# Strassen's seven half-size products for the gate and up products of a SwiGLU FFN, on one core

## The chip, the cores and the metric

The kernel runs on one core of one Trainium2 chip. The metric is the device time of one execution in microseconds (us); a time given for a kernel is the median of its runs. The engines are named as in the profile: PE is the matrix engine's matmuls, PEld its weight loads, DVE the vector engine, ACT the scalar engine, POOL the GpSimd engine, SP the engine that issues the DMAs here.

## The reference

The program is a trunk of two pre-norm residual layers over one sequence of 1024 tokens with 1024 channels, all in float32. Layer 0 is a Mamba-2 mixer, layer 1 a causal Conformer convolution module; a dense SwiGLU FFN with 2816 hidden channels follows each, and a norm ends the stack.

```python
def swiglu_ffn(u, w_gate, w_up, w_down):
    return (jax.nn.silu(u @ w_gate) * (u @ w_up)) @ w_down

h = x
h = h + mamba2_mixer(rmsnorm(h, ssm_norm), ...)
h = h + swiglu_ffn(rmsnorm(h, ffn_norm[0]), ffn_w_gate[0], ffn_w_up[0], ffn_w_down[0])
h = h + conformer_conv_module(rmsnorm(h, cv_norm), ...)   # two products around a 31-tap depthwise convolution
h = h + swiglu_ffn(rmsnorm(h, ffn_norm[1]), ffn_w_gate[1], ffn_w_up[1], ffn_w_down[1])
return rmsnorm(h, final_norm)
```

## The kernel before

Activations lie with channels on the 128 partitions and tokens along the free dimension. The sequence is cut into two blocks of T = 512 tokens, block 0 and block 1; the residual `h` of each is eight tiles of [128, 512]. Every large product is taken in three fast passes: `split` (L183 to L186) writes a number as a rounded part `hi` (ACT, L185) and the rest `lo` (a subtraction on DVE, or on POOL where `weng` says so, L186), and `gemm` (L206 to L211) adds lo x hi, hi x lo and hi x hi into one PSUM bank. Both the activations (`norm_u` makes `U[b]`, eight pairs) and the weights are split on the chip; `weight` (L188) fetches a tile into one of two staging buffers `wst` through SP's queue and splits it into `whi` and `wlo`, four buffers each.

The FFN is cut into parts. `ffn(l, f0, nf, blocks)` stands for `nf` hidden tiles of 128 channels from tile `f0` of layer `l`. Its first steps are the gate and up products, a pair of steps for each hidden tile: 24 matmuls of 512 columns for each block, then SiLU, product and a split into `hid`. Its last eight steps are the down products, 3 x nf matmuls for each block and output tile `d`, added into `h` at L682; for a block in `done` the square of `h` is added to a running sum for the next norm. `chain` strings parts together: the down products of a part stand behind the first two steps of the next part. The very last part cuts its down products into two token halves, so its matmuls have 256 columns.

SBUF space is given out by hand: `Slots` holds 15 big buffers [128, 4, 512] (8 KB a partition) and 6 small ones, taken from a list in the order in which they were given back. PSUM has eight banks; `bank` deals them out in turn by use.

The order of the work is a list `q` of steps (`Unit`), written out by hand in `run` with `weave` and `put`: first the mixer's eight stages with the input and output projections of other stages between, then FFN parts, the convolution module of block 0 with FFN parts of block 1 as filler (the convolution itself is DVE's work, 31 taps, `conv31`), the module of block 1 with layer 1's FFN of block 0 as filler, and the rest of the FFN, in which the blocks share the weights of some parts. `emit` walks the list. A step's weights are fetched and split one step ahead (`AHEAD`), at a higher priority (`BOOST`). A list scheduler then sets each engine's instruction order before the program runs, from priorities and its own estimate of times; the engines run their queues in that order, held back by semaphores alone.

```python
        c = self.chain((0, 8, 5, [0]), (0, 13, 5, [0]), (0, 0, 4, [0, 1]), (0, 4, 4, [0, 1], [0]))
        q += put(c, *at(n1, (1, 3, 3, 4, 4)))
        n0 = self.norm_u(0, "cv_norm")
```

A norm (`norm_u`, `rstd_a`, `rstd_b`) sums the running squares over the partitions by matmuls of one column (L245), takes the root and the reciprocal on small tiles, spreads them by a product (L269), and then makes the eight tiles of `U[b]` one after the other on DVE (L298) and ACT.

Of the kernel before, what the change touches and what calls it, by code (L numbers as in the profile page):

```python
# [36 lines left out]
NBIG = 15  # L37
# [3 lines left out]
NR = 2  # L41


class Slots:
# [6 lines left out]
    def new(self, name, dt=F32):  # L51
        i = self.free.popleft()
        self.cnt += 1
        t = self.pool.tile(self.shape, dt, tag=f"{self.prefix}{i}", name=f"{name}_{self.prefix}{self.cnt}")
        self.own[id(t)] = (i, t)
        return t

    def drop(self, *ts):
        for t in ts:
            i, _ = self.own.pop(id(t))  # L60
            self.free.append(i)


class Unit:
    """A step of the program: `load` fetches its weights and may be emitted ahead of `run`."""

    def __init__(self, run, load=None):
        self.run, self.load, self.then = run, load, None


def weave(main, fill):
    """The units of `main` in order, with the units of `fill` spread evenly between them."""
# [9 lines left out]
def put(q, *at):  # L82
    """The units of q, with others put in before the given places."""
# [9 lines left out]
def at(units, places):  # L93
    """Pairs for `put`: each unit with its place; the last place is for all that are left."""
# [3 lines left out]
class Trunk:  # L98
    def __init__(self, ctx, tc, io):
# [5 lines left out]
        self.big = Slots(self.cp, "b", NBIG, [P, 4, T])  # L105
        self.small = Slots(self.cp, "s", NSMALL, [P, T])
# [22 lines left out]
    def consts(self):  # L129
        nc, cp = self.nc, self.cp  # L130
        self.par = cp.tile([P, PAR_N], F32, name="par")
# [9 lines left out]
        # le[k, l] = 1 where k <= l; gtr[k, s] = 1 where k > s  # L141
        self.le = cp.tile([P, P], F32, name="le")
# [4 lines left out]
        self.gtr = cp.tile([P, P], F32R, name="gtr")  # L147
        nc.vector.tensor_copy(self.gtr, gt)
        self.small.drop(tmp)
    def selects(self):  # L150
        nc, cp = self.nc, self.cp
        # sel[32 g + h, (q, p)] = 1 where h == q, for the 8 heads of group g
        self.sel = cp.tile([P, 8, 64], F32R, name="sel")
# [9 lines left out]
    def halves(self):  # L163
        nc, cp = self.nc, self.cp
        # halves of the convolution's weights and of the gate norm: silu is taken through tanh
        self.cw = cp.tile([P, 120], F32, name="cw")
# [3 lines left out]
        self.gh = cp.tile([P, 16], F32, name="gh")  # L170
# [3 lines left out]
    def warm(self, n):  # L174
        """Has TensorE's clock up by the time that the first inputs are there."""
# [12 lines left out]
    def weight(self, src, kk, cols=P, into=None):  # L188
        """Loads a [128, kk, cols] tile of weights and splits it, into a big tile if given; returns per-k (hi, lo)."""
# [75 lines left out]
    def rstd_b(self, dg, tag="ss", nz=NZ):  # L265
        """Those diagonals on all partitions: a PSUM bank."""
# [9 lines left out]
    def norm_u(self, b, gname, g0=0, keep=None, pool=()):  # L276
        """u = rmsnorm(h) * g of block b, split into self.U[b]; the factors also go to `keep`, if given."""
# [27 lines left out]
    def raw_u(self, b, gname):  # L305
        """x * g of block b, split, for the products that run ahead of the norm."""
# [16 lines left out]
    # ---------------------------------------------------------------- mixer  # L323
# [11 lines left out]
    def mixer_setup(self):  # L335
# [8 lines left out]
        self.mix_bigs = [self.c_am, self.c_em, self.c_xd, self.c_H, self.c_bc, self.c_ms]  # L344
# [648 lines left out]
```

## Time and profile before

| | before |
|---|---|
| median of 3 runs | 2612.21 us (2611.63 to 2615.15) |
| profiled execution, its span | 2612.1 us |
| median of the runs less that span | 0.1 us |
| PE busy, mean granted clock | 2585.7 us, 0.997 |
| DVE, ACT, POOL busy | 1683.8, 1034.9, 479.8 us |
| matmuls | 11922 |
| data read and written in HBM | 201.86 and 4.19 MB |

The span runs from the first to the last instruction; of the profiled execution no other time is recorded, and what lies around the span is taken as the difference to the median. A busy share is that of the whole span. In a row of a group stand the line, engine and operation, the tile written and the tiles read, the shape, the count, the busy time with the mean of one in ns, and the idle time of the engine ahead of them with what ended it. In a row of a list in order of time stand the start and the duration in us; matmuls are pipelined, so their pace is read from start to start. In the chain of waits each step leads back from what ended last to what released it.

### The profile page before, as it was taken

To read this page: it belongs to the slowest core of one execution; us is meant where nothing else is said; L and a number is where in the kernel's file an instruction comes from. 1 tells how busy PE (TensorE), PEld (TensorE's weight loads), DVE (VectorE), ACT (ScalarE), POOL (GpSimd) and SP (SyncE) were. 2 spreads that over 40 slices of the span, in tenths; PEclk is the share of its full clock that TensorE was granted. 3 is DMA by queue.
4 is the path that set the end of the run, shared out by engine and by line. 5 is a ranking of instruction groups with operands and counts; after the bars stand their busy time and mean duration, and the time that the engine had idled before them with its cause. 6 is when DMAs were issued, how large, how long until landed. Compare 5 with 4: busy or idle time off the path is not lost.

```text
span 2612.1 us, 31342 instructions
## 1 busy us (share of the span) xinstructions
PE 2585.7 (99%) x11922; PEld 2087.3 (80%) x11922; DVE 1683.8 (64%) x2681; ACT 1034.9 (40%) x1865; POOL 479.8 (18%) x441
## 2 busy tenths in 40 slices
PE   8999999999999999999999999999999999999998
PEld 6777887888887888888888888878888888888887
DVE  7888889888889554323258993679995522235335
ACT  5554565555555343221233333543325322123232
POOL 3214211112111000000004444444444000000000
PEclk9999999999999999999999999999999999999999
DMA  4222222222222323211113232222232311113322
GB/s 143 81 65 73 73 60 81 73 73 73 81 65 69 94 88 100 79 41 56 37 61 99 96 97 93 92 91 95 90 98 91 94 55 39 53 57 105 96 92 87
DMA packets 69702, 208.07 MB, mean 80 GB/s; under 512 B 7728, under 2 KB 10032, under 8 KB 69552
## 3 DMA queue, kind: packets, MB, share of 16 engines
q1 hardware_dynamic: 69552, 206.08, 25.3%
q8 instruction: 93, 1.52, 0.3%
q14 instruction: 57, 0.47, 0.1%
HBM read 201.86 MB, written 4.19 MB: 79 GB/s over the span
## 4 chain that ended last, share of the span: by engine, by line
PE 93%; DVE 5%; issue 1%; ACT 0%; DMA 0%; POOL 0%; SPq 0%; DVEq 0%; ACTq 0%
PE p L210 87%; DVE wlo L186 1%; PE p L573 1%; PE p L577 1%; PE p L565 1%; DVE v_s L450 1%; PE p L245 1%; PE p L529 0%; PE p L538 0%; PE p L539 0%; PE p L269 0%; PE p L555 0%; DVE un_s L298 0%; PE p L509 0%; DVE ulo_b L186 0%
## 5 line engine op out<-in xcount | busy, mean ns | idle before, releaser
L185 ACT ACTIVATE whi<-wst 128x512 fp32r<-128x512 f32 (+1 forms) x764 | 470.9, 617 | 1141.3 <-PE p L210 1016.7
L210 PE MATMUL p<-uhi_b,wlo 128*128 128x512 f32 x2296 | 917.0, 400 | 0.6 <-ACT uhi_b L185 0.6
L210 PE MATMUL p<-ulo_b,whi 128*128 128x512 f32 x2296 | 906.1, 395 | 1.3 <-POOL ulo_b L186 1.2
L210 PE MATMUL p<-uhi_b,whi 128*128 128x512 f32 x2296 | 906.3, 395 | 0.0
L186 DVE TENSOR_TENSOR wlo<-wst,whi 128x512 fp32r<-128x512 f32 (+2 forms) x524 | 368.2, 705 | 405.0 <-ACT whi L185 401.0
L210 PEld LDWEIGHTS p<-ulo_b,whi 128*128 128x128 f32 x2296 | 432.2, 188 | 105.2 <-issue 3.0
L210 PEld LDWEIGHTS p<-uhi_b,wlo 128*128 128x128 f32 x2296 | 431.6, 188 | 105.1 <-issue 4.0
L210 PEld LDWEIGHTS p<-uhi_b,whi 128*128 128x128 f32 x2296 | 432.1, 188 | 101.3 <-issue 0.2
L186 POOL TENSOR_TENSOR wlo<-wst,whi 128x512 fp32r<-128x512 f32 x240 | 309.6, 1290 | 885.6 <-ACT whi L185 884.0
L210 PE MATMUL p<-hid_b,whi 128*128 128x512 f32 x1296 | 405.6, 394 | 0.0
L210 PEld LDWEIGHTS p<-hid_b,whi 128*128 128x128 f32 x1296 | 243.4, 188 | 56.7
L210 PE MATMUL p<-hid_b,wlo 128*128 128x512 f32 x648 | 255.1, 394 | 0.0
L682 DVE TENSOR_TENSOR h<-h,p 128x512 f32<-128x512 f32 (+1 forms) x144 | 94.5, 656 | 129.6 <-PE p L210 129.3
L666 DVE TENSOR_TENSOR sg_s<-sg_s,p 128x512 f32<-128x512 f32 x88 | 60.4, 687 | 182.4 <-PE p L210 182.4
L746 DVE SCALAR_TENSOR_TENSOR p<-ci_b,par,p 128x503 f32<-128x503 f32 (+28 forms) x240 | 160.1, 732 | 0.9
L748 DVE SCALAR_TENSOR_TENSOR p<-ci_b,par,p 128x512 f32<-128x512 f32 x232 | 158.0, 747 | 0.3
L210 PEld LDWEIGHTS p<-hid_b,wlo 128*128 128x128 f32 x648 | 121.8, 188 | 28.1
L450 DVE SCALAR_TENSOR_TENSOR v_s<-raw,cw,v_s 128x512 f32<-128x512 f32 x144 | 110.8, 772 | 3.7 <-ACT v_s L448 2.4
L522 POOL TENSOR_TENSOR am_b<-le,dtr 128x512 fp32r<-128x512 f32 x64 | 80.1, 1270 | 173.6 <-PE p L539 172.3
L210 PE MATMUL p<-yh_b,wlo 128*128 128x512 f32 x256 | 106.7, 417 | 0.0
L210 PE MATMUL p<-yh_b,whi 128*128 128x512 f32 x256 | 101.3, 396 | 0.0
L210 PE MATMUL p<-yl_b,whi 128*128 128x512 f32 x256 | 101.2, 395 | 0.0
(192 smaller groups left out, 2466.7 us busy)
## 6 DMA issues: line engine op xcount, KB each, us to landing
wst<-w_gu SPq DMA_DIRECT2D x144, 512.0 KB, 3.6
wst<-w_in SPq DMA_DIRECT2D x80, 512.0 KB, 3.7
wst<-w_pw SPq DMA_DIRECT2D x48, 512.0 KB, 3.6
wst<-w_dn SPq DMA_DIRECT2D x48, 448.0 KB, 3.3
wst<-w_out SPq DMA_DIRECT2D x64, 256.0 KB, 2.6
wst<-w_dn SPq DMA_DIRECT2D x40, 256.0 KB, 2.6
wst<-w_dn SPq DMA_DIRECT2D x16, 320.0 KB, 2.9
h<-xT SPq DMA_DIRECT2D x16, 256.0 KB, 6.3
```

The lines of the kernel that those rows point to most:

```text
L185: self.nc.scalar.activation(hi, src, AF.Copy)
L186: (eng or self.nc.vector).tensor_tensor(lo, src, hi.bitcast(F32), ALU.subtract)
L210: self.nc.tensor.matmul(acc, a, b, start=n == 0, stop=n == tot - 1)
L245: nc.tensor.matmul(st[:, z:z + 1], s[:, z * P:(z + 1) * P], self.ones[:, :1], start=True, stop=True)
L450: nc.vector.scalar_tensor_tensor(v, raw[:, k:k + T], w(k), v, op0=ALU.mult, op1=ALU.add)
L522: nc.gpsimd.tensor_tensor(r4(amh), lb, self.ah[:, z, h4].unsqueeze(2).to_broadcast([P, 4, P]), ALU.mult)
L565: nc.tensor.matmul(O[:, zs(j)], H[:, zs(j)], CT[:, zs(z)], start=True, stop=True)
L573: nc.tensor.matmul(Y[po:po + 64, zs(hh // 2)], self.XDT[z % 2][:, hh * 64:(hh + 1) * 64], E[:, zs(r)], start=True, stop=True)
L666: nc.vector.tensor_tensor(t, t, W.pop(("acc", b, 1)), ALU.mult)
L682: nc.vector.tensor_tensor(h, h, acc, ALU.add)
L746: nc.vector.scalar_tensor_tensor(acc[:, s:], x[:, :T - s], w(s), acc[:, s:], op0=ALU.mult, op1=ALU.add)
L748: nc.vector.scalar_tensor_tensor(acc if s < 30 else c, x[:, T - s:2 * T - s], w(s), acc, op0=ALU.mult, op1=ALU.add)
```

## The change

For a pair of hidden tiles, one block and one of gate and up, the product is [256 hidden x 1024 channels] by [1024 channels x 512 tokens]. Cut in two along each of the three directions it is a 2 x 2 by 2 x 2 block product. Before, it is taken as eight block products (64 K-steps of 128 and 3 passes: 96 matmuls of 512 columns for gate and up together). `seven` takes it as seven products of 128 hidden channels, 512 channels and 256 tokens: 7 x 12 matmuls of 256 columns. The sums of weight blocks are made on POOL for each such product (`sums`), those of the inputs once for a block and a layer (`sums_u`), and the results are put together on DVE from four PSUM banks. Weights and sums are split after the sums are made. The weights of the seven products come in one fetch of 1 MB to a big buffer (`fetch`), and each of `fetch`, `sums`, `w1` to `w4` is placed a given time ahead of the product that needs it: `Unit` gets an estimate `t` of its PE time, and `emit` sorts these early steps in by it (12 x 0.119 us for a product).

27 pairs of hidden tiles are taken in this way, in parts of four tiles (one part of two): layer 0, tiles 0 to 17 of block 0 and 0 to 7 of block 1; layer 1, tiles 14 to 21 of block 0 and 2 to 21 of block 1. The others stay as they were. Parts no longer serve two blocks at once. The order changes with it: block 0's FFN of layer 0 ends ahead of the convolution module, block 1's last parts of it come after the module of block 0, and layer 1's order for the two blocks follows. The norms of the next step are put between the last 16 down products of a chain.

For space there are 17 big buffers and three of half size [128, 4, 256]; the mixer's constants and small tiles move into two of the big buffers, which are given back after the mixer; the convolution's input is kept for one block with a border of 30 columns (`HALO`) instead of both blocks; and the memory set aside for DMA descriptors is 1024 bytes. The layout of `w_gu` in HBM puts the four blocks of a pair side by side.

The diff, cut to its core:

```diff
-NBIG = 15
+NBIG = 17
+NHALF = 3
...
+    def sums_u(self, b):
...
+        def join():
+            st["R"] = [self.big.new("rs"), self.big.new("rs")]
+            for q, r in enumerate(st["R"]):
+                h, l = self.UB[b][2 * q:2 * q + 2]
+                nc.gpsimd.tensor_tensor(r, h.bitcast(F32), l.bitcast(F32), ALU.add)
+            self.TU[b], self.TB[b] = {}, []
...
+        def first():
+            r0, r1 = st["R"]
+            tt(r0[:, :, lo], r0[:, :, lo], r0[:, :, hi], ALU.subtract)
+            nc.gpsimd.tensor_tensor(r0[:, :, hi], r0[:, :, hi], r1[:, :, hi], ALU.subtract)
+            stt(r1[:, :, hi], r0[:, :, lo], -1.0, r1[:, :, hi], op0=ALU.mult, op1=ALU.subtract)
+            tt(r1[:, :, lo], r1[:, :, lo], r1[:, :, hi], ALU.add)
+            keep("t4", r1[:, :, lo])
...
+    def seven(self, b, src, name, done):
...
+        def fetch():
+            W["q"] = self.big.new("wq")
+            nc.sync.dma_start(W["q"].rearrange("p a t -> p (a t)"), src.rearrange("p a k c -> p (a k c)"))
+
+        def sums():
+            q, s = W["q"], self.big.new("ws")
+            W["s"] = s
+            a21 = q[:, 2:3].to_broadcast([P, 2, T])
+            nc.gpsimd.tensor_tensor(s[:, 0:2], q[:, 0:4:3], a21, add)
+            nc.gpsimd.tensor_tensor(s[:, 2], q[:, 0], s[:, 1], add)
+            nc.gpsimd.tensor_tensor(s[:, 3], q[:, 1], s[:, 2], add)
+
+        def pair(n0, n1, x):
+            w = self.big.new("wh", F32R)
+            self.split(w[:, 0:2], w[:, 2:4], x)
...
+        def w1():
+            pair("a11", "a22", W["q"][:, 0:4:3])
...
+        def w3():
+            pair("s3", "s1", W["s"][:, 0:2])
+
+        def w4():
+            pair("s2", "s4", W["s"][:, 2:4])
...
+        def p1():
+            for n in "abcd":
+                A[n] = self.bank2()
+            product("a11", "b11", A["a"][:, :HT])
...
+            nc.scalar.activation(A["v"], A["a"][:, :HT], AF.Copy)
+
+        def p4():
+            product("a22", "t4", A["b"][:, HT:])
+
+        def p7():
+            product("s3", "n3", A["c"][:, :HT])
+
+        def p6():
+            product("s2", "t2", A["b"][:, :HT])
+            tt(A["v"], A["v"], A["b"][:, :HT], add)
+            tt(A["w"], A["c"][:, :HT], A["v"], sub)
+
+        def p5():
+            product("s1", "t1", A["d"][:, :HT])
+            A["x"] = self.half.new("hx")
+            tt(A["x"][:, 3], A["w"], A["d"][:, :HT], sub)
+
+        def p2():
+            product("a12", "b21", A["a"][:, :HT], True)
+            tt(A["x"][:, 2], A["w"], A["b"][:, HT:], add)
+
+        def p3():
+            product("s4", "b22", A["d"][:, :HT], True)
+            tt(A["x"][:, 1], A["v"], A["d"][:, :HT], add)
+            self.small.drop(A.pop("s"))
+            done(A["a"][:, :HT], A["x"])
+        t = 12 * MH
+        return [Unit(p1, t=t, pre=((14, fetch), (9, sums), (4.5, w1))), Unit(p4, t=t),
+                Unit(p7, t=t, pre=((4.5, w3),)), Unit(p6, t=t, pre=((4.5, w4),)), Unit(p5, t=t),
+                Unit(p2, t=t, pre=((4.5, w2),)), Unit(p3, t=t)]
...
+        def up(f, c11, y):
+            b = blocks[0]
+            x = W.pop(("x", f))
+            nc.vector.tensor_tensor(x[:, 0], x[:, 0], c11, ALU.mult)
+            nc.vector.tensor_tensor(x[:, 1:], x[:, 1:], y[:, 1:], ALU.mult)
...
+            self.split(t[:, 0:2], t[:, 2:4], xv)
...
-        c = self.chain((0, 8, 5, [0]), (0, 13, 5, [0]), (0, 0, 4, [0, 1]), (0, 4, 4, [0, 1], [0]))
-        q += put(c, *at(n1, (1, 3, 3, 4, 4)))
+        c = self.chain(fast(0, 0, 4, [0]), fast(0, 4, 4, [0]), fast(0, 8, 4, [0]), fast(0, 12, 4, [0]),
+                       fast(0, 16, 2, [0], [0]), free=0, hold=8)
+        q += put(c, *at(n1, (-16, -14, -12, -10, -8)))
...
+        q += put(p2, *at(self.sums_u(1), (1, 2, 3)))
+        n0 = self.norm_u(0, "ffn_norm", 8)
+        c = self.chain(fast(0, 0, 4, [1]), fast(0, 4, 4, [1], [1]), free=1, hold=8)
+        q += put(c, *at(n0, (-16, -14, -12, -10, -8)))
...
+        c = self.chain(fast(1, 14, 4, [0]), fast(1, 18, 4, [0], [0]), free=0, hold=8)
+        q += put(c, *at(n1, (-16, -14, -12, -10, -8)))
...
+        c = self.chain(self.ffn(1, 0, 2, [1]), fast(1, 2, 4, [1]), fast(1, 6, 4, [1]), fast(1, 10, 4, [1]),
+                       fast(1, 14, 4, [1]), fast(1, 18, 4, [1], [1], True), free=1, hold=1)
+        su = self.sums_u(1)
+        q += put(c, (0, f0[:1]), (1, f0[1:] + su[:1]), (2, su[1:2]), (3, su[2:]), (-7, f1[:1]), (-5, f1[1:])) + f2
...
-    nc = _bacc.Bacc("TRN2", target_bir_lowering=False, num_devices=1)
+    nc = _bacc.Bacc("TRN2", target_bir_lowering=False, num_devices=1, dynamic_dma_scratch_size=1024)
```

More of the change, by code (lines that the diff above doesn't have):

```diff
@@ L41 @@
 NR = 2
+HALO = 30
+TW = HALO + T
+HT = T // 2
+MM = 0.2315
+MH = 0.119
 class Slots:
@@ L51, in new @@
     def new(self, name, dt=F32):
+        assert self.free, [x[2] for x in self.own.values()]
         i = self.free.popleft()
@@ L105, in __init__ @@
         self.big = Slots(self.cp, "b", NBIG, [P, 4, T])
+        self.half = Slots(self.cp, "x", NHALF, [P, 4, HT])
         self.small = Slots(self.cp, "s", NSMALL, [P, T])
@@ L644, in ffn @@
+    def ffn(self, l, f0, nf, blocks, done=(), halves=False, fast=False):
         nc = self.nc
@@ L668, in gu, with gate @@
                 self.small.drop(t)
+        def gate(f, c11, x):
+            W["x", f] = x
+            nc.scalar.activation(x[:, 0], c11, AF.Silu)
+            nc.scalar.activation(x[:, 1:], x[:, 1:], AF.Silu)
+        def up(f, c11, y):
[3 more added lines that the diff above has]
+            nc.vector.tensor_tensor(x[:, 1:], x[:, 1:], y[:, 1:], ALU.mult)
+            t = self.big.new("hid", F32R)
+            hid[b].append(t)
+            xv = x.rearrange("p (m n) c -> p m (n c)", n=2)
+            self.split(t[:, 0:2], t[:, 2:4], xv)
+            self.half.drop(x, y)
         def load_dn(d):
@@ L814, in run @@
                 self.big.drop(*self.LB[b])
-        return [Unit(lambda d=d: run(d), lambda d=d: load(d)) for d in range(KD)]
+        return [Unit(lambda d=d: run(d), lambda d=d: load(d), 24 * MM) for d in range(KD)]
     def final(self, b, part=()):
```

197 lines of the change are left out of this document (136 added, 61 removed).

## The prediction

> **What bounds the kernel now.** I read the page first: the busy shares and the slices, then the shares of the chain of waits.
>
> ```profile
> PE 2585.7 (99%) x11922; PEld 2087.3 (80%) x11922; DVE 1683.8 (64%) x2681; ACT 1034.9 (40%) x1865; POOL 479.8 (18%) x441
> ...
> PE   8999999999999999999999999999999999999998
> PEclk9999999999999999999999999999999999999999
> ...
> PE 93%; DVE 5%; issue 1%; ACT 0%; DMA 0%; POOL 0%; SPq 0%; DVEq 0%; ACTq 0%
> PE p L210 87%; DVE wlo L186 1%; PE p L573 1%; PE p L577 1%; PE p L565 1%; DVE v_s L450 1%; PE p L245 1%; PE p L529 0%; PE p L538 0%; PE p L539 0%; PE p L269 0%; PE p L555 0%; DVE un_s L298 0%; PE p L509 0%; DVE ulo_b L186 0%
> ...
> L210 PEld LDWEIGHTS p<-ulo_b,whi 128*128 128x128 f32 x2296 | 432.2, 188 | 105.2 <-issue 3.0
> ```
>
> TensorE is busy from end to end at the full granted clock, and 87% of the chain is one helper, `gemm` at L210. A busy PE need not be PE at its peak, so next come the longest pieces of the chain in order of time (start, us, what), then one stretch of PE's own list whose matmuls are half as wide, with what follows it, then two stretches of the busy times by window.
>
> ```profile
> 930.77 417.42 PE p L210 x1800
> ...
> 1355.15 273.14 PE p L210 x1176
> ```
>
> ```profile
> 2559.37 22.61 PE L210 MATMUL p<-hid_b,wdn_b 128*128 128x256 f32 x189
> 2581.82 0.50 PE L245 MATMUL p<-onesr,ssum_s 128*128 128x1 f32 x4
> ```
>
> ```profile
> 840.00:1355.00 515.00, 515.00 (x2232) 417.79 (x2231) 208.03 (x336) 145.31 (x244) 0.00 (x0) 1.00 0.23 70
> ...
> 1735.00:1970.00 235.00, 235.00 (x1011) 189.46 (x1010) 207.64 (x307) 76.69 (x126) 110.62 (x86) 1.00 0.30 94
> ```
>
> 1800 matmuls of 512 columns in 417.42 us and 1176 in 273.14 are 0.232 us each. The 189 of 256 columns fill the time to the next instruction, (2581.82 - 2559.37) / 189 = 0.1188 us each. These runs have no hole, so in the FFN a matmul's price is its pace. The windows show the cover: DVE busy 208 of 515 us in the first FFN stretch, and 208 of 235 us under the block-1 convolution, both without PE idling. So nothing but PE is saved or lost here, unless another engine comes late.
>
> **The change, part by part.**
>
> Matmuls. A plain pair of hidden tiles for one block takes 2 tiles x 2 (gate, up) x 24 matmuls = 96 of 512 columns: 96 x 0.232 = 22.27 us. By the seven products it takes 2 x 7 x 12 = 168 of 256 columns: 168 x 0.1188 = 19.96 us. The new order has 27 such pairs: 9 of layer 0 on block 0, 4 on block 1, then 4 and 10 of layer 1. Removed are 2592 wide matmuls (601.3 us), added 4536 narrow ones (538.9 us): -62.4 us. The last part, which is cut in token halves, shrinks from seven hidden tiles to four: 144 narrow matmuls become 72 wide ones, 17.1 against 16.7 us, -0.4 us.
>
> What feeds a seven. One `seven` is 7 x 12 x 0.1188 = 9.98 us of PE. Its other work is priced from these groups (last columns: busy, mean ns) and rows in order of time (start, duration).
>
> ```profile
> L682 DVE TENSOR_TENSOR h<-h,p 128x512 f32<-128x512 f32 x128 | 87.8, 686 | 119.7 <-PE p L210 119.6
> ...
> L682 DVE TENSOR_TENSOR h<-h,p 128x256 f32<-128x256 f32 x16 | 6.7, 419 | 9.9 <-PE p L210 9.8
> ```
>
> ```profile
> 1360.52 2.72 DVE L298 SCALAR_TENSOR_TENSOR un_s<-h,par,p 128x512 f32<-128x512 f32 x4
> ...
> 1363.75 2.49 DVE L186 TENSOR_TENSOR ulo_b<-un_s,uhi_b 128x512 fp32r<-128x512 f32 x4
> ```
>
> ```profile
> L185 ACT ACTIVATE whi<-wst 128x512 fp32r<-128x512 f32 x704 | 443.8, 631 | 1078.2 <-PE p L210 960.3 <-POOL wlo L186 56.0 <-issue 53.4
> ...
> L185 ACT ACTIVATE whi<-wst 128x128 fp32r<-128x128 f32 x20 | 6.1, 310 | 11.1 <-PE p L210 10.2 <-DMA wst<-w_dt 0.2
> ```
>
> ```profile
> 1653.78 1.28 POOL L186 TENSOR_TENSOR wlo<-wst,whi 128x512 fp32r<-128x512 f32 x1 [1.85 <-ACT whi L185]
> 1655.76 1.02 POOL L186 TENSOR_TENSOR wlo<-wst,whi 128x384 fp32r<-128x384 f32 x1 [0.70 <-ACT whi L185]
> ```
>
> A DVE op of 512 columns follows the last after (2.49 - 0.69) / 3 = 0.60 us (0.66 for the scaled form at 1360.52), and a column costs (686 - 419) / 256 = 1.04 ns: 0.33 us for 256 columns, 0.87 for 768, 1.13 for 1024. POOL's column costs (1.28 - 1.02) / 128 = 2.03 ns, so 2.32 us for 1024. ACT's is (631 - 310) / 384 = 0.84 ns, 1.06 us for 1024. Per seven: DVE splits weights (3 of 1024, one of 512: 3.99 us), makes five sums that read PSUM (1.65), and every second seven multiplies 256 and 768 columns and splits 1024 of `hid` (2.33, half is 1.17): 6.8 us. POOL makes the weight sums, 2.32 + 2 x 1.28 = 4.9 us. ACT: 3 x 1.06 + 0.63 for weights, 0.42 for the copy, half of 0.42 + 0.85 + 1.06: 5.4 us. Each is below 9.98, so at full overlap the sevens cost nothing more. But the two SBUF users meet:
>
> ```profile
> 1659.24 1.30 POOL L186 TENSOR_TENSOR wlo<-wst,whi 128x512 fp32r<-128x512 f32 x1 [2.46 <-ACT whi L185]
> ...
> 1669.27 1.30 POOL L186 TENSOR_TENSOR wlo<-wst,whi 128x512 fp32r<-128x512 f32 x1 [1.84 <-ACT whi L185]
> ```
>
> ```profile
> 1655.70 1.28 DVE L790 TENSOR_TENSOR co_b<-co_b,p 128x512 f32<-128x512 f32 x2
> ...
> 1659.89 1.20 DVE L186 TENSOR_TENSOR ll_b<-co_b,lh_b 128x512 fp32r<-128x512 f32 x1
> ...
> 1669.74 1.37 DVE L186 TENSOR_TENSOR ll_b<-co_b,lh_b 128x512 fp32r<-128x512 f32 x1 [1.17 <-ACT lh_b L185]
> 1671.04 0.67 DVE L682 TENSOR_TENSOR h<-h,p 128x512 f32<-128x512 f32 x1
> ```
>
> At 1659.24 and 1669.27 POOL subtracts. DVE's subtraction of two SBUF tiles that begins meanwhile takes 1.20 and 1.37 us instead of 0.69 and ends 0.55 us behind POOL, while the one that reads PSUM (1655.70, two in 1.28 us) overlaps POOL's 1655.76 unharmed. So DVE's two-SBUF-input work, 3.99 + half of 0.87 + 1.13 = 5.0 us a seven, and POOL's 4.9 us take turns: 9.9 of 9.98 us. The Trainium skill ("SBUF — State Buffer", Who interferes with whom) says that the later of two such instructions is blocked until the first is through; the trace agrees, with the 1.37 us. Without that rule DVE would have 3.2 us spare in each seven, the stall below would be near nothing and the sum 2556; with it as the rows show, the sum is the 2575 below.
>
> What is queued behind such a wait: DVE takes its queue in order, and `p3` (bank `d`) may not add to its bank before DVE has read `p5`'s result from it (`x[:, 3]`). Only `p2`, 1.43 us, lies between. DVE is in a two-input op for 5.0 of 9.98 us, and about half of these meet POOL; then the read waits on average half of POOL's 2.32 us, half of DVE's 1.13, and its own 0.33, some 2.0 us, 0.6 past the cover: 0.25 x 0.6 = 0.15 us. I add 0.2 us for weights that reach `p1`, `p7` or `p6` late in the same way (they are called 4.5 us ahead and need 1.06 + 1.13 plus one block): 0.35 us a seven. Bounds: 0, as in the window where DVE is 88% busy and PE never idles; and DVE and POOL strictly in turn, 6.8 + 4.9 = 11.7, 1.7 us a seven. I stay near the lower, dense row. 54 sevens x 0.35 = +19 us (0 to 92).
>
> Loads. Each seven fetches one 1 MB block where 512 KB tiles came before.
>
> ```profile
> wst<-w_gu SPq DMA_DIRECT2D x144, 512.0 KB, 3.6
> ...
> wst<-w_dn SPq DMA_DIRECT2D x40, 256.0 KB, 2.6
> ```
>
> From 2.6 us at 256 KB and 3.6 at 512, 1 MB is some 5.6 us by estimate, and it is issued 14 us ahead, 5 ahead of POOL's sums. Gate/up traffic goes from 144 x 512 KB to 54 x 1 MB and 68 x 512 KB, since block 0 and 1 no longer share splits: 16 MB more; w_dn goes from 104 to 160 issues, 8 MB more. All go through SP's queue, where a fetch waits for a big buffer and the w_dn loads behind it: of 17, inputs and their sums hold 8, `hid` 2, weights up to 6, so one or two are free. At 4.5 to 14 us of lead I put this at 0; if a buffer comes 5 us late the sums do too, which is part of the 1.7 us bound.
>
> Norms. Two waits of the old order go. In its chain between 1655 and 1725:
>
> ```profile
> 1655.53 19.42 PE p L210 x84
> ...
> 1674.97 0.70 DVE h L682
> ...
> 1675.69 0.64 ACT sq_s L223
> ...
> 1676.35 1.23 DVE ssum_s L231
> ...
> 1677.63 1.05 PE p L245 x8
> ...
> 1721.77 0.76 DVE h L811
> ...
> 1724.43 1.05 PE p L245 x8
> ```
>
> PE's products end at 1655.53 + 19.42 = 1674.95, and PE stands until 1677.63 behind the last sum of squares; it stands again from about 1721.75 to 1724.43. Each is 2.7 us, so -5.4 us: the new order has other work between. It has three like places: after the last w_dn product of block 0 and 1 in layer 0 and of block 0 in layer 1, a norm comes at once. A wait there is 0.60 + 0.64 + 0.60 plus hand-overs, 2.1 us. Two I take at that, +4.2 (0 if the matmuls of the next unit are put ahead). The first is worse, because the part ahead of it has two hidden tiles only: 8 w_dn units of 6 matmuls, 11.1 us of PE, against 8 x (0.33 + 0.60 + 0.60) = 12.2 us of DVE. Before these lie 8 units of 12 (22.3 us), with DVE at 2.33 + 8 x 1.20 and the block-1 norm, about 2.6 + 8 x 1.26: 24.6 us. Then come two plain units (11.1 us; DVE 2.4). DVE reaches 39.2 us where PE stands at 44.5, and now the cv norm: 2 us for the sum, the steps that the end of the kernel shows as
>
> ```profile
> 2601.49 0.61 PE L245 MATMUL p<-onesr,ssum_s 128*128 128x1 f32 x4 [1.42 <-DVE ssum_s L231]
> ...
> 2605.07 3.22 DVE L831 SCALAR_TENSOR_TENSOR h<-h,par,p 128x256 f32<-128x256 f32 x8 [0.68 <-PE p L269]
> ```
>
> 3.6 us, then 8 x 1.26: 54.9. The first pw1 product wants its last input at 44.5 + 4.9 (seven eighths of 24 x 0.232) = 49.4, so it is 5.5 us late: +6 (0 to 12).
>
> `sums_u`: POOL joins 2 x 2048 columns (some 9 us), DVE and POOL some 15 more, three times. Twice it lies under 45 us of w_out or pw2; in the last chain under 22 us of plain units with block 0's final norm: +2 (0 to 8). Cover gone, each would cost its 24 us. Constants in two big tiles, the 30-column halo copies (16 on POOL), the convolution moved with its FFN filler: no more work on PE, hidden as the convolution is now; 0, and its cover is the 88%-busy window.
>
> Sum, on the profiled span (2612.1 us, which the median of the runs exceeds by 0.1, so nothing is added around it): -62.4 - 0.4 - 5.4 + 19 + 4.2 + 6 + 2 = -37.0, so **2575 us**.
>
> **The rivals.**
> Slower: DVE and POOL in turn on the shared port. For it: 9.9 of 9.98 us are claimed, and both queues are in order. Against: PSUM readers escape, and the 22 us of w_dn between four sevens let DVE catch up. 54 x 1.7 = 92 in place of 19: 2648. It decides from (37 + 19) / 54 = 1.04 us a seven on. The Trainium skill's page named above speaks for this one. Chance 0.15.
> Halfway: 0.7 to 1.13 us a seven, 2594 to 2617. Chance 0.15, about half of it above 2607.
> All hidden: no new wait; -62.4 - 0.4 - 5.4: 2544, up to 2556 with a few. For it: the 88% window. Chance 0.15.
> The narrow matmuls don't hold 0.1188 us: if every 188 ns weight load showed, 4536 x 0.188 - 601.3 = +251.5 and 2870 us. Against it: the 189 had loads of 188 ns too. Chance 0.03.
> My forecast, 0.1 to 0.7 us a seven: 2556 to 2594. Chance 0.52.
>
> **How the numbers follow.** 0.2% (5 us) is what a measurement can tell. Faster: 0.52 + 0.15 + 0.08; same: 0.07; slower: 0.15 + 0.03. The range 2546 to 2617 drops the two slow cases and a little of the fast one, 0.2 in all; the likeliest's own is 2556 to 2594.
>
> **What the profile would show.** PE's instructions up by 1872, 4536 + 192 matmuls of 128x256 at 0.119 us from start to start. Right: no piece of the FFN chain longer than 0.5 us that isn't PE. Wrong: DVE or POOL in the chain at `seven`'s sums and splits, PE waiting for DVE ahead of `p3`, POOL's adds well over 2.3 us; a hole over 10 us at the first pw1; whi/wh waiting for a DMA.

## The result, and the profile after

| | before, run beside it | after |
|---|---|---|
| median | 2612.03 us (2611.63 to 2615.15) | 2752.73 us (2751.0 to 2754.5) |
| ratio to before | | 1.0533 [1.0519, 1.0548] |
| span of the profiled execution | 2612.1 us | 2752.0 us |
| mean granted clock | 0.997 | 0.966 |

The changed kernel is 141 us slower; 2575 was forecast, faster, with 2617 as the upper end. The page of the changed kernel, the lines that answer to those of before (busy shares, the slices of PE and its clock, the chain by engine and by line, then one issue group):

```profile
PE 2586.6 (94%) x13794; PEld 2191.6 (80%) x13794; DVE 2123.9 (77%) x3072; ACT 1175.8 (43%) x1993; POOL 863.7 (31%) x623
...
PE   8999999999998898889999998999999988998887
PEclk9999999999999999999999998999999999999999
...
PE 71%; DVE 18%; issue 4%; POOL 3%; ACT 3%; DMA 1%; SPq 0%; DVEq 0%; POOLq 0%; ACTq 0%
PE p L226 54%; PE p L749 11%; DVE wh_b L202 5%; DVE wlo L202 2%; POOL ws_b L717 1%; ACT wh_b L201 1%; DVE hid_b L202 1%; DVE v_s L465 1%; DMA wq_b<-w_gu 1%; PE p L588 1%; POOL ws_b L718 1%; PE p L592 1%; PE p L580 1%; DVE em_b L603 1%; DVE un_s L314 1%
...
wq_b<-w_gu SPq DMA_DIRECT2D x54, 1024.0 KB, 4.8
```

PE executes the 1872 instructions more that were foretold, and its share falls from 99% to 94%. DVE rises from 5% of the chain to 18%. `gemm` is now L226, the sevens' product L749. PE is idle for 2752.0 - 2586.6 = 165.4 us, against 26.4 before. Who ends that idle time, from the table of waits of PE (total us, times, longest):

```profile
PE p L749 <- DVE hx_x L776: 104.3, 27, 6.1
PE p L285 <- DVE dgh_s L277: 7.1, 5, 3.0
```

L776 is DVE's read of `p5`'s result (`x[:, 3]`), which `p3` needs before it may use bank `d` again. In 26 of the 27 pairs PE waits for it once, each time at `p3` of the first of the pair's two sevens, for 2.0 to 6.1 us; the 27th wait that is counted, at the `p3` of a second seven, is 0.2 us long. No other wait comes near. One such wait, in order of time (start, duration, idle before and who ended it); first PE, whose `p2` began at 1059.90 and should be followed at once by `p3`:

```profile
1059.90 0.28 PE L749 MATMUL p<-uhi_b,wlo 128*128 128x256 f32 x1
...
1061.21 0.28 PE L749 MATMUL p<-uhi_b,whi 128*128 128x256 f32 x1
1064.64 0.58 PE L749 MATMUL p<-uhi_b,wh_b 128*128 128x256 f32 x1 [3.15 <-DVE hx_x L776]
1065.02 0.41 PE L749 MATMUL p<-ulo_b,wh_b 128*128 128x256 f32 x1
1065.23 0.63 PE L749 MATMUL p<-uhi_b,wh_b 128*128 128x256 f32 x2
...
1067.36 0.47 PE L226 MATMUL p<-hid_b,wlo 128*128 128x512 f32 x1
...
1089.73 0.28 PE L749 MATMUL p<-uhi_b,wh_b 128*128 128x256 f32 x1
```

DVE and POOL in the same stretch:

```profile
1055.73 2.82 DVE L202 TENSOR_TENSOR hid_b<-hx_x,hid_b 128x1024 fp32r<-128x1024 f32 x1 [1.39 <-ACT hid_b L201]
1058.47 2.32 DVE L202 TENSOR_TENSOR wh_b<-wq_b,wh_b 128x1024 fp32r<-128x1024 f32 x1
1060.71 2.30 DVE L202 TENSOR_TENSOR wh_b<-ws_b,wh_b 128x1024 fp32r<-128x1024 f32 x1
1062.93 0.41 DVE L770 TENSOR_TENSOR vw_s<-vw_s,p 128x256 f32<-128x256 f32 x1
...
1064.17 0.41 DVE L776 TENSOR_TENSOR hx_x<-vw_s,p 128x256 f32<-128x256 f32 x1
```

```profile
1055.05 2.41 POOL L717 TENSOR_TENSOR ws_b<-wq_b 128x1024 f32<-128x1024 f32 x1 [14.47 <-DMA wq_b<-w_gu]
1057.54 2.16 POOL L718 TENSOR_TENSOR ws_b<-wq_b,ws_b 128x512 f32<-128x512 f32 x1
1059.78 2.14 POOL L719 TENSOR_TENSOR ws_b<-wq_b,ws_b 128x512 f32<-128x512 f32 x1
```

The two engines alternate to the end of the chain of adds: POOL until 1057.46, DVE's first split until 1058.55, POOL until 1059.70, DVE until 1060.79, POOL until 1061.92, DVE until 1063.01. Each split takes 2.3 to 2.8 us in place of 1.2 (e2 below), and behind the third stand the four small operations that end with L776. `p6` had ended at about 1058.45 (36 matmuls of 0.119 us from 1054.17), so L770, which adds its result, is 4.5 us late. Of what stands ahead of it, two operations are not urgent: the weight splits (`wh_b`) are for the seven that begins at 1089.73, as the current one, which ends at 1067.36, had the last of its weights split by 1046.0. The static order has put them there, 30 us early.

After the pause the matmuls stand 0.21 us apart instead of 0.12 (1065.02 to 1065.23). The windows show the clock (us, PE busy, ..., PEclk, DMA share, GB/s):

```profile
1044.20:1061.30 17.10, 17.10 (x146) 17.08 (x144) 11.25 (x13) 4.87 (x7) 6.09 (x3) 1.00 0.38 139
1061.30:1064.60 3.30, 0.19 (x2) 0.00 (x0) 3.23 (x6) 1.85 (x3) 0.62 (x1) 0.93 0.00 0
1064.60:1069.00 4.40, 4.36 (x19) 4.12 (x20) 2.14 (x3) 0.85 (x1) 1.35 (x1) 0.67 0.21 60
1069.00:1085.00 16.00, 16.00 (x70) 12.93 (x70) 9.81 (x12) 5.81 (x8) 4.51 (x3) 1.00 0.23 66
```

After 3.3 us without a matmul the granted clock is 0.67 on average over the next 4.4 us: 0.50 from 1064.6 to 1067.3, and 1.00 again from 1067.8 on. So a wait costs more than its own length. The Trainium skill ("TensorE: Matmul & The Clock Gate", Part 1) says that an idle window of about 3.4 us brings the clock down to half, and that a matmul then takes its columns over 1.2 GHz, which for 256 is 0.213 us; the trace agrees, with 0.21 us, after a pause a little shorter. The length of the pause alone does not decide it here. In the changed kernel a pause from 2234.8 to 2236.7, which is 2.0 us, was followed first by 1.5 us at the full clock and then by 3.2 us at 0.50; in f3 below, one of 2.7 us that ended at 1719.9 was followed by none (1.00 from 1717 to 1725).

### The profile page after: what moved, and what is told of

It is laid out like the page before. It is cut to its first block, busy times and chain, and to the rows that moved or that the text cites. A ratio compares the mean times of both kernels' runs of the same rounds, so it can differ in the third digit from the quotient of the medians.

```text
span 2752.0 us, 35952 instructions
## 1 busy us (share of the span) xinstructions
PE 2586.6 (94%) x13794; PEld 2191.6 (80%) x13794; DVE 2123.9 (77%) x3072; ACT 1175.8 (43%) x1993; POOL 863.7 (31%) x623
## 3 DMA queue, kind: packets, MB, share of 16 engines
q8 instruction: 108, 1.77, 0.3%
## 4 chain that ended last, share of the span: by engine, by line
PE 71%; DVE 18%; issue 4%; POOL 3%; ACT 3%; DMA 1%; SPq 0%; DVEq 0%; POOLq 0%; ACTq 0%
PE p L226 54%; PE p L749 11%; DVE wh_b L202 5%; DVE wlo L202 2%; POOL ws_b L717 1%; ACT wh_b L201 1%; DVE hid_b L202 1%; DVE v_s L465 1%; DMA wq_b<-w_gu 1%; PE p L588 1%; POOL ws_b L718 1%; PE p L592 1%; PE p L580 1%; DVE em_b L603 1%; DVE un_s L314 1%
## 5 line engine op out<-in xcount | busy, mean ns | idle before, releaser
L201 ACT ACTIVATE whi<-wst 128x512 fp32r<-128x512 f32 (+3 forms) x644 | 395.9, 616 | 834.7 <-PE p L226 631.1
L226 PE MATMUL p<-uhi_b,wlo 128*128 128x512 f32 x1432 | 576.1, 403 | 9.8 <-POOL wlo L202 5.3
L226 PE MATMUL p<-ulo_b,whi 128*128 128x512 f32 x1432 | 566.4, 396 | 2.4 <-POOL ulo_b L202 1.2
L226 PE MATMUL p<-uhi_b,whi 128*128 128x512 f32 x1432 | 565.6, 395 | 0.0
L226 PE MATMUL p<-hid_b,whi 128*128 128x512 f32 x1344 | 423.9, 397 | 0.8 <-DVE hid_b L202 0.8
L226 PEld LDWEIGHTS p<-uhi_b,wlo 128*128 128x128 f32 x1432 | 271.4, 190 | 76.9 <-POOL wlo L202 7.0
L226 PEld LDWEIGHTS p<-ulo_b,whi 128*128 128x128 f32 x1432 | 271.2, 189 | 67.4 <-DVE ulo_b L202 3.2
L226 PEld LDWEIGHTS p<-uhi_b,whi 128*128 128x128 f32 x1432 | 271.0, 189 | 61.4 <-issue 0.2
L749 PE MATMUL p<-tu_b,wh_b 128*128 128x256 f32 x2592 | 317.3, 282 | 0.0
L749 PEld LDWEIGHTS p<-tu_b,wh_b 128*128 128x128 f32 x2592 | 313.3, 191 | 0.0
L749 PE MATMUL p<-uhi_b,wh_b 128*128 128x256 f32 x864 | 209.2, 331 | 104.3 <-DVE hx_x L776 104.3
L226 PEld LDWEIGHTS p<-hid_b,whi 128*128 128x128 f32 x1344 | 256.6, 191 | 58.2 <-DVE hid_b L202 1.1
L226 PE MATMUL p<-hid_b,wlo 128*128 128x512 f32 x672 | 268.4, 399 | 6.0 <-DVE un_s L314 3.2
L749 PEld LDWEIGHTS p<-uhi_b,wh_b 128*128 128x128 f32 x864 | 172.6, 237 | 110.3 <-DVE hx_x L776 109.8
L202 DVE TENSOR_TENSOR wh_b<-ws_b,wh_b 128x1024 fp32r<-128x1024 f32 x108 | 181.7, 1683 | 81.3 <-ACT wh_b L201 81.2
```

The lines of the kernel that those rows point to most:

```text
L201: self.nc.scalar.activation(hi, src, AF.Copy)
L202: (eng or self.nc.vector).tensor_tensor(lo, src, hi.bitcast(F32), ALU.subtract)
L226: self.nc.tensor.matmul(acc, a, b, start=n == 0, stop=n == tot - 1)
L749: nc.tensor.matmul(to, x, y, start=n == 0 and not more, stop=n == 11, skip_group_check=True)
```

## The experiments

All times are medians of the kernel's runs; ratios are to the kernel before, on the same chip. Beside the four groups of runs (the change, e, f with g1, h) the kernel before took 2612.0, 2613.5, 2611.8 and 2612.3 us, so a difference of 2 us between runs of different groups means nothing.

**e1: the new order and space, with plain products**

```diff
-        fast = lambda *a, **k: self.ffn(*a, fast=True, **k)
+        fast = lambda *a, **k: self.ffn(*a, fast=False, **k)
         # and the units of sums_u are left out
```

> The changed kernel with its new order, SBUF plan and weight layout, but with plain products (eight half blocks as 24 matmuls of 512 columns) in place of every seven, and without the sums of inputs. Theory (the loss sits in the sevens alone): the new order costs only its norms, so 2612 plus or minus 15 us, clock 0.99, no PE wait of more than 3 us in the FFN. Rival (the new order, the unshared weights and the tighter SBUF lose it): 2680 us or more.

2599.79 us, ratio 0.9949 [0.9934, 0.9964]. As expected, the order, the halo and the space are not the loss; they gain some 14 us. No wait went for it: PE's idle time is 27.4 us (2598.8 - 2571.4), against 26.4 before, and its busy time fell from 2585.7 to 2571.4. What made these matmuls shorter is open.

**e2: POOL reads no weights.** The sums of weight blocks are left out; POOL writes a constant in their place.

```diff
-            nc.gpsimd.tensor_tensor(s[:, 0:2], q[:, 0:4:3], a21, add)
+            nc.gpsimd.memset(s[:, 0:2], 0.01)
             # the two sums of 512 columns likewise
```

> The sums of weight blocks are left out: POOL fills the same buffers with a constant, so it reads no SBUF in a seven, and the DVE queue keeps its order nearly everywhere. All else is as in the changed kernel. Theory (POOL's adds and DVE's two-input splits block each other on the shared port, DVE comes 3 to 5 us late to the read that p3 waits for, and the pause drops the clock): the 1024-column splits fall from 1.68 us mean to about 1.23, the wait of PE for L776 from 104 us to under 25, the clock rises to 0.99, time 2555 to 2600 us. Rival (DVE is late because splits for later sevens stand ahead in its queue, and wait there for fetches that come late; the port adds little): the wait stays over 70 us and the time over 2690 us.

2575.37 us, ratio 0.9853 [0.9838, 0.9867]: as expected, and 177 us less than the change. The matmuls are the same, and DVE's 3072 instructions, read in order of time, have the same line, tiles and shape at all but 83 places. The groups of 1024-column splits in the changed kernel (last columns: busy, mean ns of one, idle before) and in this one:

```profile
L202 DVE TENSOR_TENSOR wh_b<-ws_b,wh_b 128x1024 fp32r<-128x1024 f32 x108 | 181.7, 1683 | 81.3 <-ACT wh_b L201 81.2
L202 DVE TENSOR_TENSOR wh_b<-wq_b,wh_b 128x1024 fp32r<-128x1024 f32 x54 | 95.5, 1768 | 16.8 <-ACT wh_b L201 16.8
```

```profile
L202 DVE TENSOR_TENSOR wh_b<-ws_b,wh_b 128x1024 fp32r<-128x1024 f32 x108 | 131.7, 1222 | 60.1 <-ACT wh_b L201 59.9
L202 DVE TENSOR_TENSOR wh_b<-wq_b,wh_b 128x1024 fp32r<-128x1024 f32 x54 | 68.1, 1261 | 15.4 <-ACT wh_b L201 15.4
```

A split falls from 1.68 and 1.77 us to 1.22 and 1.26, and the wait at L776 is gone. PE's idle time falls from 165.4 to 51.5 us and its busy time, for equal matmuls, from 2586.6 to 2524.2:

```profile
PE 2524.2 (98%) x13794; PEld 2137.6 (83%) x13794; DVE 1990.3 (77%) x3072; ACT 1173.5 (46%) x1993; POOL 624.9 (24%) x623
```

So the 176.3 us between the two spans are 113.9 of standing still (104.3 of them the wait at L776) and 62.4 of slower matmuls.

**e3 and e4: `p3` in a bank of its own**, in e4 together with e2's edit (the weight sums left out). It costs one more DVE sum and one more bank a seven.

```diff
-            for n in "abcd":
+            for n in "abcde":
...
             tt(A["x"][:, 3], A["w"], A["d"][:, :HT], sub)
+            tt(A["x"][:, 1], A["v"], A["d"][:, :HT], add)
...
-            product("s4", "b22", A["d"][:, :HT], True)
-            tt(A["x"][:, 1], A["v"], A["d"][:, :HT], add)
+            product("s4", "b22", A["e"][:, :HT])
+            tt(A["x"][:, 1], A["x"][:, 1], A["e"][:, :HT], add)
```

> p3 gets a PSUM bank of its own (five banks a seven instead of four) and one more 256-column DVE sum adds p5's result, so p3 no longer waits for DVE to read bank d. Nothing else is taken away; port and queue are as they were. Theory (this one wait, with the half clock behind it, is the whole loss): about 104 us of waits and 80 us of lost clock come back, 2560 to 2610 us. Rival (DVE and POOL are too slow for the sevens, so the wait moves to the next place, weights for p1 and p7 or banks not read yet): 2660 us or more, with as much PE idle time under other names.

> Both edits: p3 in its own bank and POOL writing constants instead of making the weight sums (these are left out). Theory: nothing is left to wait for in the sevens, so the arithmetic gain shows: 2545 to 2575 us, clock 0.99. Rival (late fetches and the norms hold it): 2600 us or more.

e3: 2625.47 us, ratio 1.0048 [1.0033, 1.0063]; e4: 2582.19, 0.9880 [0.9864, 0.9897]. Both expectations were missed: e3 lies between its theory and its rival, and e4 is 7 us above its range. In e3 POOL still holds DVE up as long as before, but PE no longer hangs on it so closely. Its split group and its largest waits:

```profile
L202 DVE TENSOR_TENSOR wh_b<-ws_b,wh_b 128x1024 fp32r<-128x1024 f32 x108 | 180.7, 1674 | 50.9 <-ACT wh_b L201 50.9
```

```profile
PE p L226 <- DVE un_s L314: 11.6, 2, 8.5
...
PE p L749 <- DVE wh_b L202: 7.1, 5, 2.8
```

The same 1.67 us splits then cost 2625.47 - 2582.19 = 43 us rather than 177. The slow splits alone are not the loss; slow splits ahead of the hand-over of one bank are. The edit itself costs 6.8 us (e4 against e2), and the traces show where: the wait of 8.5 us at `un_s` above is the norm behind block 0's FFN, it stands in e4 too (at 1221.3) and in f2, and in e2 PE waits there for less than 2 us. Why the new plan leaves that hole was not traced.

**f1 and f2: the weight sums on DVE**, in f2 with e3's bank.

```diff
-            nc.gpsimd.tensor_tensor(s[:, 0:2], q[:, 0:4:3], a21, add)
-            nc.gpsimd.tensor_tensor(s[:, 2], q[:, 0], s[:, 1], add)
-            nc.gpsimd.tensor_tensor(s[:, 3], q[:, 1], s[:, 2], add)
+            tt(s[:, 0:2], q[:, 0:4:3], a21, add)
+            tt(s[:, 2], q[:, 0], s[:, 1], add)
+            tt(s[:, 3], q[:, 1], s[:, 2], add)
```

> The three sums of weight blocks of each seven move from POOL to DVE; nothing is left out. DVE's own work in a seven rises by 2.3 us to about 9.1 of 9.98. Theory (the shared port, not DVE's amount of work, makes p3 wait): splits of 1024 columns near 1.25 us, PE's wait for L776 under 40 us, clock 0.985 or more, time 2585 to 2635 us. Rival (DVE is simply too full in the sevens): waits of 80 us or more, time over 2670 us.

> The sums on DVE, and p3 in a bank of its own, so that PE no longer waits for the read behind p5 (one more 256-column DVE sum, 9.5 of 9.98 us). Theory: with the port free and the tight wait gone, only input sums and norms are left, 2580 to 2610 us, which beats the kernel before (2612) and perhaps the new order with plain products (2600). Rival (DVE's amount of work binds now): 2630 us or more, PE waiting for weight splits.

f1: 2575.65 us, ratio 0.9863 [0.9848, 0.9878]; f2: 2582.31, 0.9885 [0.9871, 0.9900]. f1 is 9 us below its expected range, f2 within it. Nothing is left out here, and the loss is gone. DVE now carries 6.8 + 1.13 + 2 x 0.60 = 9.1 of 9.98 us a seven by the prediction's prices, and PE does not wait: first block 0's sevens of layer 0 in f1, from the first to the last, then the same stage in the changed kernel (window and us, then PE, PEld, DVE, ACT, POOL busy, PEclk; 1804 of PE's instructions in each):

```profile
914.50:1161.70 247.20, 247.20 (x1804) 233.66 (x1802) 195.07 (x286) 102.37 (x140) 0.00 (x0) 1.00 0.30 98
```

```profile
923.00:1229.50 306.50, 267.39 (x1804) 252.12 (x1803) 197.27 (x236) 102.45 (x140) 104.17 (x50) 0.92 0.24 79
```

So the amount of DVE's work was never the bound. (The scheduler plans anew for f1 and mixes the sums between the reads; in e2, whose order is nearly that of the changed kernel, the loss is gone too.) A run that moves only the read at L776 ahead of the two weight splits, with POOL's sums as they are, was not made; the part that the order plays is read from the rows above and from e3.

**f3: POOL's sums in eight pieces of 256 columns**

```diff
-            nc.gpsimd.tensor_tensor(s[:, 0:2], q[:, 0:4:3], a21, add)
+            for i in range(2):
+                for c in (slice(0, HT), slice(HT, T)):
+                    nc.gpsimd.tensor_tensor(s[:, i, c], q[:, 3 * i, c], q[:, 2, c], add)
             # the other two in halves too
```

> POOL's weight sums in eight pieces of 256 columns instead of one of 1024 and two of 512, with the same columns in all. Theory (each two-input DVE split waits for the POOL instruction that holds the port): a wait ends after some 0.8 us instead of up to 2.4 us, so the splits' mean falls from 1.68 to about 1.45 us and half of the loss against the kernel before comes back: 2660 to 2710 us. Rival (the total time that POOL holds the port decides, and eight pieces hold it longer): no change or slower, 2745 us or more.

2727.45 us, ratio 1.0446 [1.0428, 1.0463], between what the theory and the rival said. A split is held up for less, 1.34 us on average, but it still meets a piece, the pieces take longer in all than the whole sums, and the wait at the read (here L779) stays. The split's group, POOL's groups in the changed kernel and in f3, and f3's largest wait of PE:

```profile
L202 DVE TENSOR_TENSOR wh_b<-ws_b,wh_b 128x1024 fp32r<-128x1024 f32 x108 | 144.3, 1336 | 154.6 <-ACT wh_b L201 154.4
```

```profile
L717 POOL TENSOR_TENSOR ws_b<-wq_b 128x1024 f32<-128x1024 f32 x54 | 145.1, 2686 | 675.6 <-PE p L749 295.3 <-DMA wq_b<-w_gu 141.8 <-PE p L226 118.0
L718 POOL TENSOR_TENSOR ws_b<-wq_b,ws_b 128x512 f32<-128x512 f32 x54 | 100.5, 1861 | 4.2
L719 POOL TENSOR_TENSOR ws_b<-wq_b,ws_b 128x512 f32<-128x512 f32 x54 | 95.5, 1768 | 4.2
```

```profile
L718 POOL TENSOR_TENSOR ws_b<-wq_b 128x256 f32<-128x256 f32 x216 | 227.7, 1086 | 586.6 <-PE p L752 238.4 <-DMA wq_b<-w_gu 120.2 <-PE p L226 113.1
L722 POOL TENSOR_TENSOR ws_b<-wq_b,ws_b 128x256 f32<-128x256 f32 x108 | 120.1, 1133 | 0.0
L720 POOL TENSOR_TENSOR ws_b<-wq_b,ws_b 128x256 f32<-128x256 f32 x108 | 82.1, 781 | 0.0
```

```profile
PE p L752 <- DVE hx_x L779: 92.4, 29, 5.1
```

POOL needs 227.7 + 120.1 + 82.1 = 430 us for the pieces, 341 for the undivided sums. Smaller pieces do not free DVE: 25 us of 177 come back.

**g1, h1, h2: the sums of the inputs.** g1 is e2 without any work in `sums_u`, so it leaves out both kinds of sums; h1 is f1 with what POOL does in `sums_u` on DVE; h2 is the changed kernel with those two alone.

```diff
-                nc.gpsimd.tensor_tensor(r, h.bitcast(F32), l.bitcast(F32), ALU.add)
+                tt(r, h.bitcast(F32), l.bitcast(F32), ALU.add)
...
-            nc.gpsimd.tensor_tensor(r0[:, :, hi], r0[:, :, hi], r1[:, :, hi], ALU.subtract)
+            tt(r0[:, :, hi], r0[:, :, hi], r1[:, :, hi], ALU.subtract)
```

> As the run without POOL reads (weight sums replaced by constants), and the sums of inputs (sums_u) are left out as well: the products read parts of the inputs in their place. The run without POOL reads was 2575 us, 24 us below the plain products in the new order, where the matmuls alone should give 62. Theory (the missing 38 us are sums_u: its POOL adds stand ahead of POOL's weight splits, and its DVE work is in the way of norms): 2540 to 2550 us. Rival (the norms after the short parts and the clock keep it): 2565 us or more.

> The weight sums on DVE as in the run of 2575.7 us, and the three POOL adds of each sums_u moved to DVE too; nothing is left out. In that run POOL's join of 2 x 2048 columns (4.6 and 5.6 us) stands between its weight splits, and PE's chain goes through it at 1441 to 1464 and twice more. Theory (it is the POOL queue that makes sums_u dear, 29 us of which 0 to 8 was foreseen): 2550 to 2562 us, no POOL wlo ahead of PE there. Rival (sums_u costs by its amount of work on DVE and ACT, wherever it stands): 2568 us or more.

> The changed kernel with sums_u on DVE, while the weight sums stay on POOL. Theory (two separate losses: the port in the sevens, some 175 us, and the POOL queue in sums_u, some 20): 2725 to 2740 us. Rival (one loss, and with the port in the way sums_u matters nothing): 2748 us or more.

g1: 2546.07 us, 0.9746 [0.9732, 0.9761]. h1: 2552.35, 0.9766 [0.9752, 0.9779]. h2: 2729.27, 1.0441 [1.0427, 1.0455]. All three came as expected. The two edits give 23.3 us in h1 (against f1) and 23.5 in h2 (against the change): the same, so they are apart from the weight sums. Left out altogether (g1 against e2) the sums give 29.3. What POOL did there is seen in f1 at the first `sums_u`, DVE's rows and POOL's in order of time, and at the second in POOL's alone:

```profile
848.94 4.94 DVE L202 TENSOR_TENSOR wlo<-wst,whi 128x512 fp32r<-128x512 f32 x1 [0.30 <-ACT whi L201]
...
855.00 4.69 DVE L202 TENSOR_TENSOR wlo<-wst,whi 128x512 fp32r<-128x512 f32 x1
```

```profile
848.80 4.53 POOL L670 TENSOR_TENSOR rs_b<-uhi_b,ulo_b 128x2048 f32<-128x2048 f32 x1 [28.18 <-DVE sz_b L623]
854.56 4.58 POOL L670 TENSOR_TENSOR rs_b<-uhi_b,ulo_b 128x2048 f32<-128x2048 f32 x1 [1.23 <-DVE yl_b L202]
```

```profile
1440.75 4.62 POOL L670 TENSOR_TENSOR rs_b<-uhi_b,ulo_b 128x2048 f32<-128x2048 f32 x1 [0.72 <-PE p L226]
1445.33 1.30 POOL L202 TENSOR_TENSOR wlo<-wst,whi 128x512 fp32r<-128x512 f32 x1
1446.58 5.58 POOL L670 TENSOR_TENSOR rs_b<-uhi_b,ulo_b 128x2048 f32<-128x2048 f32 x1
1452.13 1.25 POOL L202 TENSOR_TENSOR wlo<-wst,whi 128x512 fp32r<-128x512 f32 x1
```

A weight split on DVE of 512 columns, 0.69 us elsewhere, meets an add of 2048 columns and takes 4.94 and 4.69 us: it ends 0.55 and 0.55 us behind POOL, as in the window of before. And at 1440 two such adds stand in POOL's queue ahead of weight splits of 1.30 us, so the weights of the product that should hide the adds come late. In f1 PE waits 7.3 us for such splits (0.8 in h1). It waits for DVE as well: behind DVE's meetings with the adds of the last `sums_u` come waits of 3.4 us at `un_s` (2189.1) and 3.4 at `ssum_s` (2217.6), and h1 has neither.

**h3 and h4: the two-tile part first**, in h3 on f1, in h4 on h1.

```diff
-        c = self.chain(fast(0, 0, 4, [0]), fast(0, 4, 4, [0]), fast(0, 8, 4, [0]), fast(0, 12, 4, [0]),
-                       fast(0, 16, 2, [0], [0]), free=0, hold=8)
+        c = self.chain(fast(0, 0, 2, [0]), fast(0, 2, 4, [0]), fast(0, 6, 4, [0]), fast(0, 10, 4, [0]),
+                       fast(0, 14, 4, [0], [0]), free=0, hold=8)
```

> The run of 2575.7 us (weight sums on DVE) with the part of two hidden tiles put first instead of last in block 0's FFN of layer 0, so that the last eight down products are 12 matmuls long and not 6. Theory (the short part leaves DVE behind ahead of the norm of the convolution module, +6 us in the prediction): 2562 to 2571 us. Rival (the wait there has another cause, the first fetches of the next plain part or the norm's own chain): 2573 us or more.

> All three edits together: weight sums and input sums on DVE and the short part first. If the gains add up: 2540 to 2556 us. If they are one and the same slack: as the better one of the two alone.

h3: 2573.85 us (2571.21 to 2574.99) against f1's 2575.65 (2573.76 to 2580.94): no difference that can be told, as the rival said. h4: 2545.71 (2544.75 to 2546.68) against h1's 2552.35 (2550.25 to 2553.37), 6.6 us less; ratio to before 0.9741 [0.9728, 0.9755]. h4 computes everything and is faster than both kernels, 67 us below the one before. The first norm behind block 0's FFN is not what it gains by. In h1's chain this norm is a stretch of short steps of many engines, from 1197.61 (1192.27 + 5.34) to 1211.57:

```profile
1192.27 5.34 PE p L226 x22
...
1211.57 18.63 PE p L226 x80
```

But PE works on other products meanwhile. Its largest wait in h1 between 1140 and 1290:

```profile
PE p L226 <- DVE ulo_b L202: 1.0, 2, 0.8
```

All its waits in that stretch are 1.2 us, the same in f1, and none in h4. From h1 to h4 PE's idle time falls by 5.1 us (37.2 to 32.1): 1.2 at this norm, 2.6 in two waits for L776 that h4 does not have; the rest I have not placed. A narrow matmul's pace can be read from a long piece of sevens in h4's chain:

```profile
1559.92 80.08 PE p L749 x672
```

## Why the prediction was wrong

The terms of the sum, beside what the runs give:

| term | predicted | measured |
|---|---|---|
| stall of the sevens | +19 (0 to 92) | +177 (the change against f1) |
| `sums_u` | +2 (0 to 8) | +23 (f1 against h1) |
| matmuls of the sevens | -62.4 | -47 (h1 against e1), all else of the sevens with it |
| order, all norms, last part | +4.4 (-0.4 - 5.4 + 4.2 + 6) | -14 (e1 against before) |

**The step that failed** is the price of the `p3` hand-over, "some 2.0 us, 0.6 past the cover: 0.25 x 0.6 = 0.15 us", and with it the 0.35 us a seven. The place, the wait and the cause were named; the size is 177 / 54 = 3.3 us a seven, twice the upper bound of 1.7, and the waits fall on one of the two sevens of a pair. Three things in it were wrong.

First, it took DVE's meetings with POOL as single and independent, an average half operation late. The trace at 1055 to 1063 shows them in a row: three adds of POOL, back to back, against three splits of DVE, back to back. Every split meets its add, and the delays add up, 1.6 + 1.1 + 1.1 = 3.8 us over the 1.22 of each, where only `p2`'s 1.43 us lay between.

Second, the bound "strictly in turn, 6.8 + 4.9 = 11.7" is a bound on throughput. It spreads the loss over the seven and supposes that DVE's work is needed when it is done. But the list had placed two splits for a seven 30 us later ahead of an urgent read of 0.41 us. With DVE 77% busy over the span, PE stood still for lack of one small operation: what stood ahead in the queue decided, not the sum of the work. e2 has nearly the same order with unhindered splits, and no such wait; it takes both, the order and the slow splits.

Third, no term stood for the clock. A wait of 3.3 us is followed by 4.4 us at 0.67 on average, and over the span 62.4 of the 176.3 us are matmuls that run slower, not waits. The prediction priced a stall at its own length.

The rival "DVE and POOL in turn on the shared port" was the right mechanism so far as the runs show it, which is the turns and not the port. It stood at 2648 us and a chance of 0.15; both were too low for the same reasons. "PSUM readers escape" was true of the reader itself (L776 takes 0.41 us) but not of its place behind those that don't. The rule of the Trainium skill named there ("SBUF — State Buffer", Who interferes with whom), that the later one is blocked until the first is through, is what the rows from 1055 to 1063 show.

**`sums_u`** is the second term that failed, +23 us where 2 (0 to 8) stood. It was counted three times, but the kernel calls it four times (POOL's add of 2048 columns runs 8 times, two a call), once more under pw2. And it was priced by its cover, "twice under 45 us of w_out or pw2". The cover was PE's, but these products need weights that POOL itself splits, and POOL was in 4.6 to 5.6 us adds ahead of them, and DVE's splits met the same adds. The text asked what hides the work and not what the hiding work needs from the same engine. PE's idle time falls by 16.1 us from f1 to h1 (53.3 to 37.2), its busy time by 6.5.

**The norms.** The -5.4 us for two waits of the old order is a misreading of the chain. Between 1674.95 and 1677.63 the chain goes through the sum of squares, but PE runs products with `lh_b` and `ll_b` for most of that time:

```profile
1676.86 0.39 PE L210 MATMUL p<-lh_b,wlo 128*128 128x512 f32 x1
1677.63 1.05 PE L245 MATMUL p<-onesr,ssum_s 128*128 128x1 f32 x8 [0.38 <-DVE ssum_s L231]
```

PE stood for 0.38 us there and for 0.37 at the other place, so there was 0.7 us to gain. The +6 (0 to 12) for the first norm lies high: PE waits 1.4 us there in the changed kernel, 2.5 in e1. The hole that this term foresaw does appear, with 8.5 us, in e3, e4 and f2, where DVE has one sum more a seven.

**What held.** PE's 1872 added instructions are there. A narrow matmul at full clock costs what it did: 672 in 80.08 us in h4 are 0.119 us each, so "every weight load shows" falls. POOL's adds "well over 2.3 us" and PE waiting ahead of `p3` were named as the signs of the other case, and both came (2.69 us, 104.3 us). Loads at 1 MB: 4.8 us, estimated 5.6, and no wait of PE is put down to one. The convolution's new place costs nothing that e1 shows. The rival "all hidden" foresaw 2544, and h4, in which DVE does all sums and the short part comes first, takes 2545.71. That is luck: the order gave 14 us where this rival had 5.8, by busy time and not by the waits that it named, and all that the sevens change gave 54 (h4 against e1) where it had 62.4. In h1 that gain is 47, 15 short of its matmuls. Of these 15, 6 go when the sums are left out (g1 against h1), and 6.6 with the short part first (h4 against h1); how far these two overlap, and where the rest is, I have not traced.

## What to carry to other kernels

Two in-order queues whose operations hold each other up need not lose just the average: where both had several in a row, as here, each was held up, and the urgent read behind them paid for all. Before work is given to an idle engine, ask whether its operations hold up those of a busy one, what the static order puts ahead of the shortest hand-over to PE, and what the operation would cost on the busier engine; here DVE at 82% took the sums in half the time and lost nothing. A hand-over with 1.4 us of cover is a risk to be priced by the longest run of work ahead of it, and a pause of PE of 2 us or more is to be priced with the slow matmuls that may follow it. A step of the chain of waits is not an idle PE: look at PE's own list before a wait is priced.

## What the runs showed of the hardware

A pause of PE of 3.3 us was followed by 2.7 us at a granted clock of 0.50, matmuls of 256 columns 0.21 us apart. One of 2.0 us was followed by 1.5 us at the full clock and then 3.2 us at 0.50, and one of 2.7 us in f3 by no slow stretch: its length alone did not decide. In the changed kernel the slower matmuls cost 62 us beside 114 us of waiting. POOL's adds cut to 256 columns took 0.78 to 1.13 us on average, those of 512 undivided 1.77 to 1.86, and 430 us against 341 in all: cutting the adds up did not make them cheaper. DVE's subtractions of two SBUF tiles took turns with POOL's adds (2.3 to 2.8 us in place of 1.22), while its read of PSUM took 0.41 us, as ever. How the two engines' turns are granted no run here shows.
